# Layer 0's ConvFFN in five groups of channel tiles instead of six, and one more block-product pair in each layer of a two-layer encoder trunk

## The chip, the cores and the metric

The kernel runs on one core of a Trainium2 chip. A core has a matrix engine (TensorE; PE in the profile, its weight loads PEld), a vector engine (VectorE; DVE), a scalar engine (ScalarE; ACT), GpSimd (POOL), and SyncE (SP), whose queue issues every DMA here. Each engine runs its own instructions in order and waits on semaphores for the others. Operands lie in SBUF, 128 partitions wide; matmuls accumulate in PSUM, eight banks of 128 x 512 float32. The metric is the device time of one execution in microseconds; lower is better.

## The reference

A trunk of two layers over 512 positions of 1024 channels, in float32. Each layer has a mixing part (a Fourier group and a windowed attention group, projected back and added to x) and a ConvFFN. The change touches the ConvFFN alone:

```python
D_MODEL = 1024; SEQ = 512; DEPTH = 2; D_FF = 2816

def dwconv_centred(h, w, bias):
    hp = jnp.pad(h, ((0, 0), (1, 1), (0, 0)))
    return hp[:, :-2] * w[0] + hp[:, 1:-1] * w[1] + hp[:, 2:] * w[2] + bias

for l in range(DEPTH):
    ...
    x = x + mix @ w_o[l]
    h = rmsnorm(x, norm2[l])
    up = dwconv_centred(h @ w_up[l], conv_w[l], conv_b[l])
    gate, val = up[..., :D_FF], up[..., D_FF:]
    x = x + (jax.nn.silu(gate) * val) @ w_down[l]
```

## The kernel before

Everything is held transposed: channels on the 128 partitions, the 512 positions along the free dimension. x is eight tiles of 128 x 512 (KT = 8). The hidden width of 2816 is 22 channel tiles (FT = 22), each with a gate half and a value half.

**Precision by splitting.** A float32 operand is split into a rounded high part and the remainder (`split`, `wsplit`: ScalarE copies the high part at line 94, VectorE subtracts at line 97). `mm3` then issues three matmuls per product of a 128 x 128 weight block, at lines 124 (high, high), 125 (low, high) and 126 (high, low). Weights come by DMA from HBM into `wraw` buffers (three of 1024 columns) and are split into `whi` and `wlo` buffers (five each of up to 512 columns).

**The up projection of a channel tile, two ways.** `up_eight` takes the gate weights and the value weights one after the other: eight blocks each, every block against 512 positions, so 48 matmuls 512 wide. `up_seven` takes both halves together as a 2 x 2 block product in Strassen-Winograd form over the positions' halves and the channels' halves: seven products of four blocks against 256 positions, 84 matmuls 256 wide. Its sums on the position side (`seven_h`) are made once per layer. Its sums on the weight side (`s1` to `s4`) are made for each tile by VectorE, two of them in place in the `wraw` buffers. All seven weight operands are split, and PSUM parts are added up by VectorE. `SEVEN[l]` lists the tiles of layer l done this way; before, 7 in layer 0 and 12 in layer 1.

**After the up projection**, for each half: multiply by the row norm `rb2`, then `conv` (ScalarE scales and adds the bias, VectorE adds the two neighbour taps at line 100). Then SiLU on ScalarE, the product on VectorE, and a split into the pair `a`, kept in `gu`.

**The down projection** works on groups of channel tiles, `GROUPS[l]`. When a group's tiles are done, `rows` gives its eight rows, one for each tile of x: load the weights of this row and group, split, nf x 3 matmuls into one PSUM bank, add into x. A group of at most four loads two rows with one DMA; a larger group loads each row by itself and splits it in two pieces. The rows of one group run beside the up projections of the next, spread by `want`; of the rows beside the last group two are held back until its last tile is done. The rows of the last group come after everything else (the tail), and in layer 0 each also starts the next layer's norm.

**Where `gu` lies.** Four pairs fit in the four `slab` buffers, four in two `pT` buffers (2560 columns each), and in layer 1 four more in `m4`. A group's place is given by `c = fi % 8` in layer 0 and `fi % 12` in layer 1.

**Beside layer 0's ConvFFN** runs `presplit`: it splits layer 1's projection weights in advance and stores both parts in HBM (`kept`). `PIECES[fi]` says how many such pieces follow tile fi; four more calls lie in the tail.

**Order.** The program gives the order of the data and the buffers; a scheduler places the instructions of each engine from its own model of their times, so rows and up projections interleave matmul by matmul. Buffers of one tag go round, and a transfer into a buffer waits on SP's queue until its last reader is done.

Lines that the steps below use: 133 (`wload`'s DMA: up weights, and down weights of larger groups), 858 (the paired down loads), 167 (stores of the pre-split), 94 and 97 (splits and additions), 100 (taps), 124 to 126 (matmuls).

Of the kernel before, what the change touches and what calls it, by code (L numbers as in the profile page):

```python
# [9 lines left out]
F32R = mybir.dt.float32r  # L10
# [6 lines left out]
P = 128  # L17
# [15 lines left out]
RATE, STEP0 = 1, 12  # L33
FFN_BANKS = ("mm", "mm", "mm", "av", "sc", "sc")

GROUPS = ([(0, 4), (4, 4), (8, 4), (12, 3), (15, 3), (18, 4)], [(0, 4), (4, 6), (10, 6), (16, 6)])

PIECES = [1, 1, 2, 1, 2, 2, 2] + [1, 3] * 7 + [3]
SEVEN = ((7, 9, 11, 13, 15, 17, 19), (7, 8, 10, 11, 12, 14, 15, 16, 18, 19, 20, 21))


def encoder_kernel(tc, t):
# [25 lines left out]
    def nm(s):  # L68
        uid[0] += 1
        return f"{s}_{uid[0]}"  # L70

    def f(x):
        return x.bitcast(F32)
# [6 lines left out]
    def psum(tag="mm"):  # L80
        return ps.tile([P, 512], F32, tag=tag, name=nm("ps"), bufs=BANKS[tag])

    def temp(n, tag, dt=F32):
        size, bufs = TEMPS[tag]
        return tp.tile([P, size], dt, tag=tag, name=nm(tag), bufs=bufs)[:, :n]

    def pair(tag, n=512):
        return temp(2 * n, tag, F32R).rearrange("p (s q) -> p s q", s=2)

    def halves(z):  # L90
        return [z[:, s, :] for s in range(2)]

    def act(out, in_, func=AF.Copy, **kw):
        return nc.scalar.activation(out, in_, func, **kw)  # L94

    def tt(out, a, b, op, eng=None):
        return (eng or nc.vector).tensor_tensor(out, a, b, op=op)  # L97

    def stt(out, a, s, b, op0, op1):
        return nc.vector.scalar_tensor_tensor(out=out, in0=a, scalar=s, in1=b, op0=op0, op1=op1)  # L100

    def split(hi, lo, src, scale=None, eng=None):

        if scale is None:
            act(hi, src)
            tt(lo, src, f(hi), ALU.subtract, eng)
        else:
            act(hi, src, scale=scale)
            stt(lo, src, scale, f(hi), ALU.mult, ALU.subtract)
# [18 lines left out]
    def wtile():  # L128
        return wp.tile([P, 1024], F32, tag="wraw", name=nm("wraw"))

    def wload(src, n, raw=None):
        raw = wtile() if raw is None else raw
        nc.sync.dma_start(raw[:, :n], src)
        return raw[:, :n]

    def wsplit(raw, eng=None, hi_eng=None):
        hi = wp.tile([P, 512], F32R, tag="whi", name=nm("whi"), bufs=5)
        lo = wp.tile([P, 512], F32R, tag="wlo", name=nm("wlo"), bufs=5)
        n = raw.shape[-1]
        if hi_eng is None:  # L140
            act(hi[:, :n], raw)
        else:
            hi_eng.tensor_copy(hi[:, :n], raw)
        tt(lo[:, :n], raw, f(hi)[:, :n], ALU.subtract, eng)
        return hi, lo

    def wchunks(src, n, step=512, eng=None):
        raw = wload(src, n)
        return [wsplit(raw[:, c:min(c + step, n)], eng) for c in range(0, n, step)]
# [58 lines left out]
    def fetch(key, n=512):  # L208
        w = [wp.tile([P, 512], F32R, tag=z, name=nm(z), bufs=5) for z in ("whi", "wlo")]
        for o, z in zip(w, kept[key]):  # L210
            nc.sync.dma_start(f(o)[:, :n], z)
        return w
# [124 lines left out]
    def norm_tile(k, g, acc):  # L337

        a = pair("act")
        split(a[:, 0, :], a[:, 1, :], x[k], scale=g[:, k:k + 1])  # L340
        add_square(acc, x[k], k == 0)
        return a
# [14 lines left out]
    def fold_wu(raw, w=None):  # L357
        w = temp(512, "tA") if w is None else w
        fold(w, raw)
        return w  # L360

    def wwhole():
        return wp.tile([P, 512], F32, tag="whi", name=nm("whi"), bufs=5)

    def load_wf(l, j, raw=None):

        raw = wtile() if raw is None else raw
        nc.sync.dma_start(raw[:, :512].rearrange("p (z c) -> p z c", z=2),
                          t["w_fold"][l, j].rearrange("p (z c) -> p z c", z=2)[:, :, :256])
        return raw  # L370

    def fold_wf(raw, w=None):

        w = temp(512, "tA") if w is None else w
        tt(w[:, :256], raw[:, :256], raw[:, 256:512], ALU.add)
        tt(w[:, 256:], raw[:, :256], raw[:, 256:512], ALU.subtract)
        nc.vector.memset(w[:1, 256:384], 0.0)
        return w
# [110 lines left out]
    for l in range(L):  # L489
# [6 lines left out]
        for grp in (1, 0):  # L496
# [26 lines left out]
            z = temp(1536, "pT").rearrange("p (b c) -> p b c", b=NB)  # L523
            n = 256 if grp else 384
# [174 lines left out]
        for kk in range(KT // 2):  # L699
            if not l:  # L700
                wu = load_wu(l, kk)
            for k in (2 * kk, 2 * kk + 1):
                if k >= 4:
                    fold_h(k)
                w = fetch(f"u{k}") if l else [fold_wu(wu[k % 2], wwhole())]
# [4 lines left out]
                for m in (0, 1, 2, 3, 4) if l else (3, 4, 0, 1, 2):  # L710
                    if m < 3:
                        mm3(pee[m][:, :258], [z[:, m * P:(m + 1) * P] for z in h], we, st, sp_)
                    else:
                        c = (m - 3) * P
# [27 lines left out]
        for stage in range(2):  # L742
# [12 lines left out]
            for m in range(3):  # L755
                o = pe[m][:, :258]
                for i in range(2):
                    a, b = (ue, tabs) if stage == 0 else (tabs, ue)
# [18 lines left out]
        for j in range(NF):  # L777
# [3 lines left out]
            w = fetch(f"f{j}") if l else [fold_wf(load_wf(l, j), wwhole())]  # L781
# [16 lines left out]
        for j in range(NF):  # L798
            stt(yf[j], yf[j], gF[:, l, j:j + 1], rbF, ALU.mult, ALU.mult)
            a = pair("slab")  # L800
# [23 lines left out]
        for mp in range(KT // 2):  # L824
            for i, w in enumerate(wo(0, mp)):
                m = 2 * mp + i
# [5 lines left out]
        for mp in range(KT // 2):  # L832
            for i, w in enumerate(wo(1, mp)):
                m = 2 * mp + i
# [14 lines left out]
        def rows(f0, nf, gu):  # L849

            last = f0 + nf == FT
            for m in range(KT):
                if nf > 4:
                    w = wchunks(t["w_down"][l, m, :, f0 * P:(f0 + nf) * P], nf * P, step=nf * P // 2)
                else:
                    if m % 2 == 0:
                        raw = wtile()[:, :2 * nf * P].rearrange("p (m c) -> p m c", m=2)
                        nc.sync.dma_start(raw, t["w_down"][l, m:m + 2, :, f0 * P:(f0 + nf) * P].rearrange("m p c -> p m c"))
                    w = [wsplit(raw[:, m % 2, :])]
                kw = -(-nf // len(w))  # L860
                nh = 2 if last and l == L - 1 and m == KT - 1 else 1
                for h in range(nh):
                    q0, q1 = h * S // nh, (h + 1) * S // nh
                    nps[0] += 1
                    o = psum(FFN_BANKS[nps[0] % len(FFN_BANKS)])[:, q0:q1]
                    for k in range(nf):
                        mm3(o, [z[:, (k % kw) * P:(k % kw + 1) * P] for z in w[k // kw]],
                            [gu[k][:, s, q0:q1] for s in range(2)],
                            k == 0, k == nf - 1)
                    tt(x[m][:, q0:q1], x[m][:, q0:q1], o, ALU.add)  # L870
                    if last and l == L - 1:
                        nc.sync.dma_start(t["out"][m, :, q0:q1], x[m][:, q0:q1])
                if last and l < L - 1:
                    nxt.append(norm_tile(m, g1[:, l + 1, :], acc))
                yield

        down = iter(())
        for f0, nf in GROUPS[l]:
            gu = []

            todo = KT - 2 if f0 + nf == FT else KT
            done = 0
            for fi in range(f0, f0 + nf):
                ys_ = []
                for z, u in enumerate((up_seven if fi in SEVEN[l] else up_eight)(l, fi, h2, ts, rb2)):
                    ys_.append(conv(l, fi + z * FT, u))

                    n = 2 * (fi - f0) + z
                    want = -(-todo * (n + 2 - n % 2) // (2 * nf)) if n % 2 or n == 0 else done
                    if nf <= 4:  # L890
                        want = done + -(-(todo - done) // (2 * nf - n))
                    for _ in range(want - done):
                        next(down, None)
                    done = want
                if fi in (3, 4):
                    ts.append(seven_h(len(ts), h2, room))
                for _ in range(PIECES[fi]):
                    next(ahead)
                act(ys_[0], ys_[0], AF.Silu)
                tt(ys_[0], ys_[0], ys_[1], ALU.mult)  # L900
                c = fi % (12 if l else 8)
                if c < 4:
                    a = pair("slab")
                elif c < 8:
                    if c % 2 == 0:
                        two = temp(2048, "pT", F32R).rearrange("p (n s q) -> p n s q", n=2, s=2)
                    a = two[:, c % 2]
                else:
                    a = pair("m4")
                split(a[:, 0, :], a[:, 1, :], ys_[0])  # L910
                gu.append(a)
            for _ in down:
                pass
            down = rows(f0, nf, gu)
        if l < L - 1:
            acc = accum()
# [93 lines left out]
```

## Time and profile before

| what | us |
|---|---|
| median of three runs (lowest, highest) | 1039.85 (1039.72, 1041.09) |
| the profiled execution | 1039.14 |
| its span, first to last instruction | 1037.4 |
| granted TensorE clock | 1.000 |
| layer 0's ConvFFN, about | 192 to 537 |
| layer 1's ConvFFN, about | 706 to 1037 |

The span is a little shorter than the execution's time; what lies around it is 1.7 us. In the rows of the profile, an instruction's group is given by its line, engine, operation and tiles (out<-in), then the shape. In a timeline a row has its start, its duration, and in brackets the idle time of its engine before it and what ended it. A PE row lasts longer than the step to the next row, since matmuls overlap, so steps between starts are the thing to read.

### The profile page before, as it was taken

What the parts mean: (1) busy time and instruction counts of PE and PEld (TensorE: products, weight loads), DVE (VectorE), ACT (ScalarE), POOL (GpSimd) and SP (SyncE); (2) the same over time, 40 slices, a digit from 0 to 9 for tenths busy, and PEclk for the clock granted to TensorE, in tenths of its full rate; (3) what the DMA queues carried; (4) which work ended last, traced back from release to release, by engine and by line L of the source; (5) the groups of instructions that cost most, each with busy time, mean ns of one, the idle gap of its engine ahead of it and who ended that gap; (6) DMA issues with size and microseconds to landing.
All of it is one profiled execution on the core that took longest, in us unless ns stands there. A gap on an engine that the chain in (4) does not pass through costs nothing.

```text
span 1037.4 us, 16244 instructions
## 1 busy us (share of the span) xinstructions
PE 1024.4 (99%) x5774; PEld 891.1 (86%) x5774; DVE 862.5 (83%) x1747; ACT 545.8 (53%) x1068; POOL 60.6 (6%) x142
## 2 busy tenths in 40 slices
PE   8999999999999999999999999999999999999998
PEld 8887778888888888888899887888888898989987
DVE  8788749799998889999759876396999998999973
ACT  5338736455555455555544595254555555555631
POOL 0004410000000000000000063000000000000000
PEclk9999999999999999999999999999999999999999
DMA  7232122355564546567766422423224232333242
GB/s 275 87 106 72 44 91 82 117 172 179 163 206 145 193 175 204 186 221 231 240 212 200 151 62 84 141 82 102 82 73 137 82 107 85 104 112 101 68 149 85
DMA packets 62341, 140.15 MB, mean 135 GB/s; under 512 B 6450, under 2 KB 20018, under 8 KB 62260
## 3 DMA queue, kind: packets, MB, share of 16 engines
q1 hardware_dynamic: 62260, 139.12, 41.9%
q8 instruction: 45, 0.74, 0.3%
q14 instruction: 36, 0.29, 0.1%
HBM read 116.02 MB, written 23.07 MB: 134 GB/s over the span
## 4 chain that ended last, share of the span: by engine, by line
PE 92%; DVE 5%; ACT 1%; DMA 1%; issue 1%; POOL 0%; DVEq 0%; ACTq 0%
PE ps L124 27%; PE ps L126 27%; PE ps L125 27%; PE ps L122 3%; PE ps L680 2%; PE ps L673 2%; PE ps L661 1%; DVE tF L100 1%; DMA wraw<-in_w_up_dram 1%; DVE wlo L97 1%; DVE tA L665 1%; PE ps L242 1%; PE ps L235 1%; PE ps L621 0%; PE ps L282 0%
## 5 line engine op out<-in xcount | busy, mean ns | idle before, releaser
L94 ACT ACTIVATE whi<-wraw 128x512 fp32r<-128x512 f32 (+1 forms) x323 | 190.7, 603 | 222.2 <-PE ps L126 130.5
L97 DVE TENSOR_TENSOR wlo<-wraw,whi 128x512 fp32r<-128x512 f32 (+1 forms) x331 | 213.1, 657 | 48.6 <-ACT whi L94 47.7
L124 PE MATMUL ps<-act,whi 128*128 128x512 f32 (+1 forms) x692 | 244.9, 355 | 0.0
L125 PE MATMUL ps<-act,wlo 128*128 128x512 f32 (+1 forms) x692 | 244.4, 355 | 0.4 <-DVE wlo L97 0.3
L126 PE MATMUL ps<-act,whi 128*128 128x512 f32 (+1 forms) x692 | 244.1, 354 | 0.0
L125 PEld LDWEIGHTS ps<-act,wlo 128*128 128x128 f32 x692 | 130.6, 189 | 19.4 <-DVE wlo L97 0.9
L124 PEld LDWEIGHTS ps<-act,whi 128*128 128x128 f32 x692 | 130.6, 189 | 18.7
L126 PEld LDWEIGHTS ps<-act,whi 128*128 128x128 f32 x692 | 130.7, 189 | 18.0
L100 DVE SCALAR_TENSOR_TENSOR tF<-tF,pb,tF 128x511 f32<-128x511 f32 x176 | 130.2, 747 | 4.8 <-ACT tF L94 4.6
L97 DVE TENSOR_TENSOR x<-x,ps 128x512 f32<-128x512 f32 (+1 forms) x97 | 64.9, 677 | 34.9 <-PE ps L126 34.5
L124 PE MATMUL ps<-slab,whi 128*128 128x512 f32 (+1 forms) x240 | 93.1, 390 | 0.7 <-ACT whi L94 0.7
L125 PE MATMUL ps<-slab,wlo 128*128 128x512 f32 (+1 forms) x240 | 91.8, 383 | 0.0
L94 ACT ACTIVATE tF<-tF,pb 128x512 f32<-128x512 f32 x88 | 71.1, 810 | 37.7 <-DVE tF L97 37.1
L126 PE MATMUL ps<-slab,whi 128*128 128x512 f32 (+1 forms) x240 | 89.7, 384 | 0.0
L124 PE MATMUL ps<-room,whi 128*128 128x256 f32 x266 | 75.6, 284 | 0.5 <-DVE tF L97 0.2
L125 PE MATMUL ps<-room,wlo 128*128 128x256 f32 x266 | 75.0, 282 | 0.0
L126 PE MATMUL ps<-room,whi 128*128 128x256 f32 x266 | 74.9, 282 | 0.0
L97 DVE TENSOR_TENSOR tF<-ps,rb 128x512 f32<-128x512 f32 (+1 forms) x85 | 52.6, 627 | 15.3 <-ACT rb L94 11.0
L124 PE MATMUL ps<-pT,whi 128*128 128x512 f32 (+1 forms) x148 | 56.9, 384 | 0.0
L125 PE MATMUL ps<-pT,wlo 128*128 128x512 f32 (+1 forms) x148 | 56.8, 384 | 0.0
L126 PE MATMUL ps<-pT,whi 128*128 128x512 f32 (+1 forms) x148 | 56.1, 384 | 0.0
L124 PEld LDWEIGHTS ps<-slab,whi 128*128 128x128 f32 x240 | 45.1, 188 | 9.8 <-ACT whi L94 0.9
(206 smaller groups left out, 1923.9 us busy)
## 6 DMA issues: line engine op xcount, KB each, us to landing
wraw<-in_w_up_dram SPq DMA_DIRECT2D x88, 512.0 KB, 3.8
kept<-tA SPq DMA_DIRECT2D x56, 256.0 KB, 3.2
wraw<-in_w_down_dram SPq DMA_DIRECT2D x32, 384.0 KB, 3.8
wraw<-in_w_down_dram SPq DMA_DIRECT2D x20, 512.0 KB, 4.0
whi<-kept SPq DMA_DIRECT2D x28, 256.0 KB, 3.1
wlo<-kept SPq DMA_DIRECT2D x28, 256.0 KB, 3.0
kept<-tA SPq DMA_DIRECT2D x32, 192.0 KB, 1.9
wraw<-in_w_o_dram SPq DMA_DIRECT2D x8, 512.0 KB, 4.3
```

The source lines that it names most:

```text
L94: return nc.scalar.activation(out, in_, func, **kw)
L97: return (eng or nc.vector).tensor_tensor(out, a, b, op=op)
L100: return nc.vector.scalar_tensor_tensor(out=out, in0=a, scalar=s, in1=b, op0=op0, op1=op1)
L122: nc.tensor.matmul(out, a[0], b[0], start=start, stop=stop, **kw)
L124: nc.tensor.matmul(out, a[0], b[0], start=start, stop=False, **kw)
L125: nc.tensor.matmul(out, a[1], b[0], start=False, stop=False, **kw)
L126: nc.tensor.matmul(out, a[0], b[1], start=False, stop=stop, **kw)
L235: nc.tensor.matmul(pt[:, 2 * b:2 * b + 2], acc[:, b * P:(b + 1) * P], ones2, start=True, stop=True)
L242: nc.tensor.matmul(pt[:, b * P:(b + 1) * P], r[:, b:b + 1].to_broadcast([P, P]), ident, start=True, stop=True)
L661: nc.tensor.matmul(sc[:, :n], qT[p][:, e, i * P:(i + 1) * P], kT[g][:, s, j0 * P:(j1 + 1) * P], start=s == 0, stop=s == 1)
L673: tr = nc.tensor.transpose(pp[:, j * P:(j + 1) * P], pr[:, j * P:(j + 1) * P], ident)
L680: pv = nc.tensor.matmul(py[64 * e:64 * e + 64, i0 * P:(i1 + 1) * P], vp[:, j, 64 * g:64 * g + 64], pT[:, half, e, b0:b0 + 2 * (i1 - i0) + ...
```

## The change

Layer 0's ConvFFN has the groups 4, 5, 4, 5, 4 in place of 4, 4, 4, 3, 3, 4, so five sets of eight down rows and not six. A row of a group of five is loaded alone (640 columns) and split as 384 and 256; the step of 384 is what groups of six had already. Tile 21 of layer 0 becomes an eighth block product, and layer 1 has thirteen instead of twelve, in other places: 7 to 9, 11 to 14 and 16 to 21, where it was 7, 8, 10 to 12, 14 to 16 and 18 to 21. Layer 0's places go by `fi % 9`: the two `pT` buffers are taken together at c == 4, hold four pairs, and the fifth pair of a group lies in the last 512 columns of both. After tile 21 two pieces of the pre-split follow and not three, so that one moves into the tail. The reads of `gu` take a list of two parts in place of one array.

```diff
-GROUPS = ([(0, 4), (4, 4), (8, 4), (12, 3), (15, 3), (18, 4)], [(0, 4), (4, 6), (10, 6), (16, 6)])
-
-PIECES = [1, 1, 2, 1, 2, 2, 2] + [1, 3] * 7 + [3]
-SEVEN = ((7, 9, 11, 13, 15, 17, 19), (7, 8, 10, 11, 12, 14, 15, 16, 18, 19, 20, 21))
+GROUPS = ([(0, 4), (4, 5), (9, 4), (13, 5), (18, 4)], [(0, 4), (4, 6), (10, 6), (16, 6)])
+
+PIECES = [1, 1, 2, 1, 2, 2, 2] + [1, 3] * 7 + [2]
+SEVEN = ((7, 9, 11, 13, 15, 17, 19, 21), (7, 8, 9, 11, 12, 13, 14, 16, 17, 18, 19, 20, 21))
...
                 if nf > 4:
-                    w = wchunks(t["w_down"][l, m, :, f0 * P:(f0 + nf) * P], nf * P, step=nf * P // 2)
+                    w = wchunks(t["w_down"][l, m, :, f0 * P:(f0 + nf) * P], nf * P, step=3 * P)
...
                         mm3(o, [z[:, (k % kw) * P:(k % kw + 1) * P] for z in w[k // kw]],
-                            [gu[k][:, s, q0:q1] for s in range(2)],
+                            [z[:, q0:q1] for z in gu[k]],
                             k == 0, k == nf - 1)
...
-                c = fi % (12 if l else 8)
+                c = fi % (12 if l else 9)
+                if c == 4:
+
+                    big = [temp(2560, "pT", F32R) for _ in range(2)]
                 if c < 4:
-                    a = pair("slab")
+                    a = halves(pair("slab"))
                 elif c < 8:
-                    if c % 2 == 0:
-                        two = temp(2048, "pT", F32R).rearrange("p (n s q) -> p n s q", n=2, s=2)
-                    a = two[:, c % 2]
+                    a = [big[c // 6][:, (2 * (c % 2) + s) * 512:(2 * (c % 2) + s + 1) * 512] for s in range(2)]
+                elif l == 0:
+                    a = [z[:, 2048:2560] for z in big]
                 else:
-                    a = pair("m4")
-                split(a[:, 0, :], a[:, 1, :], ys_[0])
+                    a = halves(pair("m4"))
+                split(*a, ys_[0])
                 gu.append(a)
```

## The prediction

> **What bounds the kernel now.** I read the busy shares and the chain first, then windows over the ConvFFN of both layers, then single rows of TensorE and VectorE. From the page, the engines' busy line and the chain of work that ended last:
>
> ```profile
> PE 1024.4 (99%) x5774; PEld 891.1 (86%) x5774; DVE 862.5 (83%) x1747; ACT 545.8 (53%) x1068; POOL 60.6 (6%) x142
> PE 92%; DVE 5%; ACT 1%; DMA 1%; issue 1%; POOL 0%; DVEq 0%; ACTq 0%
> ```
>
> TensorE holds 92% of the chain. The question is what it waits for inside the ConvFFN, the only part that the change touches. The windows (us; busy time of PE, PEld, DVE, ACT, POOL; clock; DMA share; GB/s) are layer 0's ConvFFN up to its last channel tile, its tail, and layer 1's tiles 18 to 21:
>
> ```profile
> 195.00:506.00 311.00, 310.14 (x1645) 268.00 (x1644) 285.16 (x510) 170.04 (x299) 0.00 (x0) 1.00 0.57 188
> 505.00:538.00 33.00, 32.87 (x164) 28.80 (x162) 23.12 (x38) 16.34 (x27) 1.10 (x6) 1.00 0.66 216
> 936.53:998.84 62.31, 62.19 (x427) 57.65 (x427) 57.56 (x105) 34.71 (x66) 0.00 (x0) 1.00 0.35 106
> ```
>
> TensorE is full in all three, at the full clock. VectorE is nearly full too: 285.16 of 311.00 us is 92%, and the same 92% in the last row. So there are two limits close together: the matmuls set the time, and VectorE may take over wherever it gets more work than the matmuls beside it cover. A busy PE hides short waits (a row lasts longer than its step to the next), so I count from start to start. Timeline of PE, wide and then narrow matmuls; 35 rows and 17 rows:
>
> ```profile
> 761.51 0.39 PE L125 MATMUL ps<-act,wlo 128*128 128x512 f32 x1
> ...
> 769.22 0.39 PE L126 MATMUL ps<-slab,whi 128*128 128x512 f32 x1
> ...
> 772.42 0.28 PE L125 MATMUL ps<-act,wlo 128*128 128x256 f32 x1
> ...
> 774.33 0.28 PE L126 MATMUL ps<-room,whi 128*128 128x256 f32 x1
> ```
>
> A wide matmul takes (769.22 - 761.51) / 34 = 0.2268 us, a narrow one (774.33 - 772.42) / 16 = 0.1194 us. A step much above these is a stall. Two of layer 0, then the five of layer 1:
>
> ```profile
> 269.50 0.39 PE L124 MATMUL ps<-slab,whi 128*128 128x512 f32 x1
> 270.01 0.38 PE L124 MATMUL ps<-room,whi 128*128 128x256 f32 x1
> ...
> 370.91 0.38 PE L124 MATMUL ps<-act,whi 128*128 128x256 f32 x1
> 371.95 0.49 PE L124 MATMUL ps<-slab,whi 128*128 128x512 f32 x1 [0.66 <-ACT whi L94]
> 372.52 0.39 PE L125 MATMUL ps<-act,wlo 128*128 128x256 f32 x1
> 372.74 0.28 PE L126 MATMUL ps<-act,whi 128*128 128x256 f32 x1
> ...
> 775.18 0.29 PE L124 MATMUL ps<-act,whi 128*128 128x256 f32 x1
> 775.74 0.38 PE L125 MATMUL ps<-act,wlo 128*128 128x256 f32 x1 [0.28 <-DVE wlo L97]
> ...
> 786.93 0.28 PE L124 MATMUL ps<-act,whi 128*128 128x256 f32 x1
> 787.45 0.39 PE L124 MATMUL ps<-room,whi 128*128 128x256 f32 x1 [0.24 <-DVE tF L97]
> ...
> 953.84 0.28 PE L126 MATMUL ps<-room,whi 128*128 128x256 f32 x1
> 954.24 0.38 PE L124 MATMUL ps<-room,whi 128*128 128x256 f32 x1
> ...
> 979.76 0.28 PE L124 MATMUL ps<-act,whi 128*128 128x256 f32 x1
> 980.03 0.39 PE L124 MATMUL ps<-room,whi 128*128 128x256 f32 x1
> ...
> 984.32 0.29 PE L124 MATMUL ps<-act,whi 128*128 128x256 f32 x1
> 984.61 0.50 PE L124 MATMUL ps<-m,whi 128*128 128x512 f32 x1
> ```
>
> At 370.91 the steps are 1.04, 0.57 and 0.22 us, which is 0.92 + 0.34 + 0.10 = 1.4 us lost; at 269.50 the step of 0.51 loses 0.3, with the 0.23 behind it 0.4. In layer 1 the five steps are 0.56, 0.52, 0.40, 0.27 and 0.29 long, so 0.44 + 0.40 + 0.28 + 0.15 + 0.17 = 1.4 us over 0.12, and with 0.10 in the step behind each 1.9 us. Two of these fall at tiles 7 and 8, three in the run of four block products 18 to 21 (0.9 us, 0.23 per tile). The stalls name splits (whi, wlo) and VectorE sums: weights that are not ready.
>
> **The change, part by part. Matmuls.** An ordinary pair is 2 x 8 x 3 = 48 wide matmuls, 48 x 0.2268 = 10.89 us. A block-product pair is 7 x 4 x 3 = 84 narrow ones, 84 x 0.1194 = 10.03 us. Each layer gets one more of these: 2 x 0.86 = **1.7 us** less TensorE time, on the path because TensorE is full. Regrouping alters no matmul: 22 tiles times 8 rows times 3 stay.
>
> [...]
>
> **VectorE's price of it.** Start to start on the DVE timeline:
>
> ```profile
> 945.08 0.68 DVE L97 TENSOR_TENSOR wlo<-wraw,whi 128x512 fp32r<-128x512 f32 x1
> 945.68 0.68 DVE L97 TENSOR_TENSOR wraw<-wraw 128x512 f32<-128x512 f32 x1
> ...
> 946.89 0.41 DVE L97 TENSOR_TENSOR tF<-tF,ps 128x256 f32<-128x256 f32 x1
> 947.22 0.75 DVE L100 SCALAR_TENSOR_TENSOR tF<-tF,pb,tF 128x511 f32<-128x511 f32 x1
> 947.88 0.69 DVE L97 TENSOR_TENSOR wlo<-wraw,whi 128x512 fp32r<-128x512 f32 x1
> ...
> 956.22 0.55 DVE L97 TENSOR_TENSOR wlo<-wraw,whi 128x384 fp32r<-128x384 f32 x1
> 956.68 0.68 DVE L97 TENSOR_TENSOR tF<-tF,tF 128x512 f32<-128x512 f32 x1
> ```
>
> So 0.60 for 512 columns, 0.46 for 384, 0.33 for 256, 0.66 for a convolution tap. An ordinary pair has 8 of the first (four weight splits, two scalings, product, last split) and 4 taps: 4.8 + 2.6 = 7.4 us. A block product has 14 (four sums, seven splits, scaling, product, last split), 5 of 256 and 4 taps: 8.4 + 1.7 + 2.6 = 12.7 us. Each conversion adds 5.3 us to VectorE, while TensorE gets shorter. ScalarE's additional splits and copies lie on an engine that is 53% busy.
>
> Layer 1, tile by tile. Beside tiles 16 to 21 runs about one down row of six channel tiles per tile: 18 wide matmuls, 4.08 us, and 2 x 0.46 + 0.60 = 1.5 us of VectorE. A block product there needs 10.03 + 4.08 = 14.1 us of TensorE and 14.2 of VectorE: about even, and the trace loses 0.23 per tile. The run grows from 18-21 to 16-21, two more at 0.23: **+0.5 us**. Beside tiles 4 to 9 run 8 rows of four over six tiles: 8 x 12 x 0.2268 / 6 = 3.6 us, VectorE 8 x 1.2 / 6 = 1.6. A block product has 13.7 against 14.3: 0.6 short. Tile 9 now follows 7 and 8 as a third: **+0.6 us**. Beside 10 to 15 the row share is 5.4 us against 2.0, so 15.5 against 14.7: covered, and the run 11 to 14 costs nothing. So layer 1 gives back about 1.1 of its 0.86: between 0 (the scheduler fills gaps) and 2 us.
>
> Layer 0. Five groups instead of six drop 8 additions into x, 8 x 0.60 = 4.8 us of VectorE. Splits go from 32 of 512 and 16 of 384 (19.2 + 7.4 = 26.6 us) to 24 of 512, 16 of 384 and 16 of 256 (14.4 + 7.4 + 5.3 = 27.1). Net 4.3 us less VectorE work in 311. Only stalls can turn this into time: 1.4 us at 370.91 and 0.4 at 269.50. The first falls at tile 13, beside rows of the old groups of three. In the new group 13 to 17 the three block products have 10.03 + 4.4 = 14.4 us of TensorE against 12.7 + 1.9 + 0.6 (one piece for the next layer) = 15.2, but the two ordinary tiles between have 15.2 against 7.4 + 1.9 + 1.8 = 11.1: 73.6 against 67.8 together, so no lasting shortage, though a local stall can appear. I take **-0.6 us**, between -1.8 (both stalls go) and +1.5 (one more like 370.91).
>
> Tile 21 of layer 0 as a block product sits before the tail. There VectorE has 23.12 of 33.00 us. Its last split ends at 511.7, and VectorE then waits for TensorE:
>
> ```profile
> 511.06 0.68 DVE L97 TENSOR_TENSOR pT<-tF,pT 128x512 fp32r<-128x512 f32 x1
> 516.17 2.48 DVE L97 TENSOR_TENSOR x<-x,ps 128x512 f32<-128x512 f32 x4 [4.43 <-PE ps L126]
> ```
>
> The 5.3 us more are partly met by this 4.4 us gap, and the two rows held back become 2 x 15 x 0.2268 = 6.8 us of cover instead of 2 x 9 x 0.2268 = 4.1. One piece of the pre-split (0.6 us on VectorE, its two stores on SP) moves from tile 21 into the same slack; if that cover failed it would cost its 0.6 us. Allocating both pT buffers at once (c == 4) waits for the previous group's rows, which are emptied before that tile begins: nothing, and 1 us at most if they ran late.
>
> Transfers. Layer 0's down weights went in 16 loads of 512 KB and 8 of 384; now 12 of 512 and 16 of 320. From the list of DMA issues (count, size, us to landing), and the waits of layer 0 (total, times, longest), ScalarE's and SP's:
>
> ```profile
> wraw<-in_w_down_dram SPq DMA_DIRECT2D x32, 384.0 KB, 3.8
> wraw<-in_w_down_dram SPq DMA_DIRECT2D x20, 512.0 KB, 4.0
> ...
> ACT whi L94 <- DMA wraw<-in_w_up_dram: 25.7, 13, 5.4
> ...
> SPq L133 <- DVE wlo L97: 57.9, 23, 6.2
> ```
>
> A 320 KB load should land in about 3.7 us (my estimate from the two sizes). A row of five holds one of three wraw buffers; a row pair held one for two rows, hence longer. I price it at nothing, covered by matmuls in the queue, and keep its failure as a rival.
>
> **Sum** on the profiled execution (1039.14 us, span 1037.4): -1.7 + 1.1 - 0.6 = -1.2, so 1037.9. The median shown, 1039.85, lies 0.7 above that execution; against it the same sum gives **1038.7 us**.
>
> **Rivals.** (1) The whole matmul gain and layer 0's relief arrive, and layer 1 hides its extra VectorE work in VectorE's idle 8%: -1.7 - 1.7 + 0.2 = -3.2, so 1036.6. For it: VectorE has 4.7 us idle in 936.53 to 998.84. Against: stalls sit exactly there. (2) VectorE takes all back: layer 1 +1.9, layer 0 unchanged: 1040.0. For it: even balance in both runs. (3) Slower: the wraw buffers. Beside tiles 9-12 and 18-21 each row now takes a load of its own; a block product holds two buffers almost to its end, so rows and the next tile's weights share the third, and SP, serving in order, holds the next up load behind a row's load that waits for a buffer. ScalarE's mean wait for an up load is 25.7 / 13 = 2.0 us. It decides once that wait outlasts the split weights TensorE still has queued; with two such waits reaching it in two of the four block products there, +4.0 on the forecast: 1042.7. Against it: SP's waits in layer 0 end with almost no stall now, and single rows in layer 1 run the same way. [...]
>
> **Chances.** About 0.2% (2.1 us) is what a measurement tells from no change. Forecast 0.42 (its own range 1037.6 to 1039.7), rival 1 0.28, rival 2 0.20, rival 3 0.10. Faster by over 0.2% (below 1037.8) is rival 1 and a little of the forecast: 0.32. Slower (above 1041.9): 0.10. The rest, 0.58, is within. The range takes rivals 1 and 2 with the stall bounds: 1036.0 to 1041.0.
>
> **What would show it.** The counts would show 168 narrow matmuls more and 96 wide ones fewer. Right: steps at layer 1's tiles 9 and 16-21 above 0.12 us, ending on wlo, whi or VectorE sums, adding about 1 us; no 1.4 us step near layer 0's tile 13; layer 0's ConvFFN shorter by 1 to 2 us. Wrong: stalls in layer 0 that end on in_w_up or in_w_down loads (rival 3), or layer 1 shorter by the full 0.86 (rival 1).

## The result, and the profile after

The changed kernel is slower: median 1054.18 us (1053.77 to 1056.23, four runs) against 1039.90 us of the kernel before in the same runs, a ratio of 1.0138 [1.0126, 1.0151]. The forecast was 1038.7 and the range ended at 1041.0. The profiled execution is 1053.77 us long, its span 1051.9.

From the page of the changed kernel, the engines' busy line and the chain that ended last:

```profile
PE 1027.7 (98%) x5846; PEld 894.2 (85%) x5846; DVE 870.5 (83%) x1769; ACT 553.4 (53%) x1088; POOL 60.3 (6%) x142
PE 79%; DVE 15%; DMA 4%; ACT 1%; issue 1%; POOL 0%; DVEq 0%; ACTq 0%
```

VectorE's share of the chain went from 5% to 15% and DMA's from 1% to 4%. To see where, I cut both spans at the row-norm matmuls (line 235) that open each ConvFFN. Windows view (us; then busy us and count of PE, PEld, DVE, ACT, POOL; granted clock; DMA share; GB/s) of the changed kernel, layer 1's ConvFFN and then layer 0's:

```profile
707.60:1051.90 344.30, 331.30 (x1979) 294.31 (x1977) 286.58 (x500) 167.42 (x302) 1.01 (x1) 1.00 0.31 94
191.50:539.70 348.20, 345.19 (x1851) 299.63 (x1850) 312.24 (x560) 192.57 (x338) 2.90 (x7) 1.00 0.59 191
```

The same view of the kernel before:

```profile
705.00:1037.40 332.40, 328.63 (x1943) 292.50 (x1941) 281.83 (x489) 166.29 (x296) 1.01 (x1) 1.00 0.32 98
191.30:537.30 346.00, 345.01 (x1817) 298.48 (x1815) 308.69 (x549) 186.00 (x324) 2.50 (x7) 1.00 0.58 191
```

Layer 0's ConvFFN is 2.2 us longer (348.2 against 346.0), layer 1's 11.9 us (344.3 against 332.4). The clock is full in all four. In layer 1 TensorE is idle for 344.3 - 331.3 = 13.0 us, where it was idle for 3.8. So the matmuls did not get slower; they wait.

For what, the waits of both kernels between 710 and 1030 us say (engine, instruction and releaser: us in total, times, longest). The changed kernel:

```profile
ACT whi L94 <- DVE wraw L97: 36.2, 17, 3.6
...
DVE sums L97 <- DMA wraw<-in_w_up_dram: 11.4, 11, 2.7
...
PE ps L124 <- DVE tF L97: 6.5, 7, 1.5
```

The kernel before:

```profile
ACT whi L94 <- DVE wraw L97: 16.3, 12, 2.5
...
DVE sums L97 <- DMA wraw<-in_w_up_dram: 3.0, 7, 0.6
...
PE ps L124 <- DVE tF L97: 0.2, 1, 0.2
```

VectorE's first operation of a block product (sums) waits four times as long for its up weights, ScalarE's splits then wait for VectorE, and TensorE at the end for VectorE. One tile shows the whole chain. Timeline of PE in the changed kernel, in the run 16 to 21, with its largest step:

```profile
973.20 0.28 PE L124 MATMUL ps<-act,whi 128*128 128x256 f32 x1
973.88 0.39 PE L125 MATMUL ps<-act,wlo 128*128 128x256 f32 x1 [0.40 <-DVE wlo L97]
...
978.05 0.28 PE L126 MATMUL ps<-act,whi 128*128 128x256 f32 x1
979.80 0.39 PE L124 MATMUL ps<-room,whi 128*128 128x256 f32 x1 [1.47 <-DVE tF L97]
```

The steps are 0.68 and 1.75 us where 0.12 is due: 0.56 and 1.63 us lost. The second ends when VectorE empties a PSUM part. VectorE's timeline there:

```profile
966.57 0.68 DVE L97 TENSOR_TENSOR tF<-tF,tF 128x512 f32<-128x512 f32 x1
969.92 0.69 DVE L97 TENSOR_TENSOR sums<-wraw,wraw 128x512 f32<-128x512 f32 x1 [2.68 <-DMA wraw<-in_w_up_dram]
...
979.34 0.41 DVE L97 TENSOR_TENSOR tF<-ps,rb 128x256 f32<-128x256 f32 x1
979.67 0.68 DVE L97 TENSOR_TENSOR wlo<-wraw,whi 128x512 fp32r<-128x512 f32 x1
```

It stood idle for 2.68 us before the tile's up weights came, and from 969.92 on has no idle time at all; what TensorE waits for stands in that queue and comes at 979.34. SP's queue says why the weights were late. Up loads of three successive tiles (x2: gate and value), the changed kernel:

```profile
947.21 1.53 SPq L133 DMA_DIRECT2D wraw<-in_w_up_dram  x2
...
963.01 1.53 SPq L133 DMA_DIRECT2D wraw<-in_w_up_dram  x2
971.11 0.33 SPq L133 DMA_DIRECT2D wraw<-in_w_down_dram  x1
980.38 1.53 SPq L133 DMA_DIRECT2D wraw<-in_w_up_dram  x2
```

The next tile's loads go out at 980.38, 0.03 us after the split that began at 979.67 ends and leaves `wraw` (979.67 + 0.68 = 980.35). This is a loop: 963.01 to 969.92 for the transfers until the sums can start (6.9 us), 969.92 to 980.35 for VectorE's queue (10.4 us), then the next load. In the 6.9 us lies about 1.2 us for which the second of the two loads, which the sums need too, waits for its own buffer (the row of both issues spans 1.53 us, a single issue 0.33). This turn takes 17.4 us, the one before it 15.8 (947.21 to 963.01); TensorE needs 14.1.

### The profile page after: what moved, and what is told of

Its sections match the earlier page's. It is cut to its first block, busy times and chain, and to the rows that moved or that the text cites. A ratio compares the mean times of both kernels' runs of the same rounds, so it can differ in the third digit from the quotient of the medians.

```text
span 1051.9 us, 16451 instructions
## 1 busy us (share of the span) xinstructions
PE 1027.7 (98%) x5846; PEld 894.2 (85%) x5846; DVE 870.5 (83%) x1769; ACT 553.4 (53%) x1088; POOL 60.3 (6%) x142
## 4 chain that ended last, share of the span: by engine, by line
PE 79%; DVE 15%; DMA 4%; ACT 1%; issue 1%; POOL 0%; DVEq 0%; ACTq 0%
PE ps L124 24%; PE ps L126 24%; PE ps L125 24%; DVE wlo L97 4%; DMA wraw<-in_w_up_dram 3%; DVE tF L100 2%; PE ps L680 2%; PE ps L673 2%; DVE tF L97 1%; PE ps L661 1%; DVE sums L97 1%; DVE wraw L97 1%; DVE act L97 1%; PE ps L122 1%; DVE x L97 1%
## 5 line engine op out<-in xcount | busy, mean ns | idle before, releaser
L94 ACT ACTIVATE whi<-wraw 128x512 fp32r<-128x512 f32 (+2 forms) x333 | 194.5, 594 | 243.9 <-PE ps L126 162.1
L97 DVE TENSOR_TENSOR wlo<-wraw,whi 128x512 fp32r<-128x512 f32 (+2 forms) x341 | 216.2, 643 | 45.7 <-ACT whi L94 44.1
L124 PE MATMUL ps<-act,whi 128*128 128x512 f32 (+1 forms) x684 | 239.5, 351 | 1.0 <-ACT whi L94 1.0
L125 PE MATMUL ps<-act,wlo 128*128 128x512 f32 (+1 forms) x684 | 239.0, 351 | 1.0 <-DVE wlo L97 1.0
L126 PE MATMUL ps<-act,whi 128*128 128x512 f32 (+1 forms) x684 | 238.5, 350 | 0.0
L124 PE MATMUL ps<-room,whi 128*128 128x256 f32 x294 | 84.8, 288 | 8.6 <-DVE tF L97 6.5
L97 DVE TENSOR_TENSOR x<-x,ps 128x512 f32<-128x512 f32 (+1 forms) x89 | 59.6, 675 | 30.1 <-PE ps L126 29.9
L125 PE MATMUL ps<-room,wlo 128*128 128x256 f32 x294 | 83.1, 282 | 0.5 <-DVE wlo L97 0.5
L126 PE MATMUL ps<-room,whi 128*128 128x256 f32 x294 | 82.9, 282 | 0.0
L124 PEld LDWEIGHTS ps<-room,whi 128*128 128x128 f32 x294 | 55.8, 190 | 12.6 <-DVE tF L97 7.0
L125 PEld LDWEIGHTS ps<-room,wlo 128*128 128x128 f32 x294 | 55.8, 190 | 1.9 <-DVE wlo L97 0.7
L126 PE MATMUL ps<-pT,whi 128*128 128x512 f32 (+1 forms) x148 | 56.8, 384 | 0.0
```

The costliest lines, as they stand in the source:

```text
L124: nc.tensor.matmul(out, a[0], b[0], start=start, stop=False, **kw)
L125: nc.tensor.matmul(out, a[1], b[0], start=False, stop=False, **kw)
L126: nc.tensor.matmul(out, a[0], b[1], start=False, stop=stop, **kw)
```

## The experiments

All ratios are medians against the kernel before in the same runs, with a 95% interval. "Layer 1" is the profiled length from line 235 to the end of the span (before 332.4, after 344.3). My theory after the result: the loss of layer 1 is that loop, three `wraw` buffers with VectorE's order in it, which a short run of block products outlives on weights loaded ahead. Rivals: VectorE simply has too much work; the new places of `gu` or the groups of layer 0 shift something later.

**Layer 1's list put back, layer 0 as changed.**

```diff
-SEVEN = ((7, 9, 11, 13, 15, 17, 19, 21), (7, 8, 9, 11, 12, 13, 14, 16, 17, 18, 19, 20, 21))
+SEVEN = ((7, 9, 11, 13, 15, 17, 19, 21), (7, 8, 10, 11, 12, 14, 15, 16, 18, 19, 20, 21))
```

> The changed kernel with layer 1's twelve block products where they were before; all else as changed. Theories for layer 1: (ring) three wraw buffers make a closed loop of load, sums, splits and release that is longer than a block-product tile's matmuls, paid once per tile of a long run; (throughput) VectorE simply has too much work in such runs; (storage) the new way of taking the pT buffers changed the order of layer 1's instructions. Ring and throughput: layer 1 as before, 331 to 333 us from its first up matmul, and the whole 2 to 3 us above before (layer 0's part): 1042 to 1043. Storage: layer 1 stays long, 1047 or more.

Measured 1044.24 us, 1.0042 [1.0027, 1.0057]; layer 1 is 332.9 us, as before. The new groups and the storage do nothing to layer 1. What is left, some 4 us, is layer 0's; about 1.5 us of it is a stretch at half clock (all four runs have a mean granted clock of 0.998; last section).

**Only layer 1's list changed, on the kernel before.** The edit is the second tuple of `SEVEN` alone.

> The kernel before with nothing changed but layer 1's list of thirteen. Ring and throughput: nearly the whole loss of layer 1, some 12 us, so 1050 to 1053. Storage: 1039 to 1041.

Measured 1051.24 us, 1.0102 [1.0085, 1.0119]; layer 1 is 346.0 us in the profiled execution, whose mean granted clock is 0.998 where the three other runs have 1.000 (last section). The list alone costs 11 us.

**The long run broken.** Tile 17 of layer 1 is made ordinary, so that 18 to 21 follow an ordinary tile as in the kernel before, and twelve block products are left.

```diff
-(7, 8, 9, 11, 12, 13, 14, 16, 17, 18, 19, 20, 21)
+(7, 8, 9, 11, 12, 13, 14, 16, 18, 19, 20, 21)
```

> The changed kernel with tile 17 of layer 1 an ordinary pair again, so twelve block products: 7 to 9, 11 to 14, 16, 18 to 21. Ring and throughput: of the 10 us of stalls in tiles 16 to 21 at most 2 remain, while those at 8, 9, 11 and 12 (about 6 us) stay: 1045 to 1047. If the number of block products mattered and not the run: 1053.

Measured 1049.02 us, 1.009 [1.0075, 1.0105], above what I had set, since layer 0 lost about 4 us in this run too. Layer 1 is 337.8 us: 6.5 less than after. Tiles 18 to 21 lose 1.8 us by their steps; in the changed kernel tiles 18 to 20 alone lose about 6. Tiles 8, 9, 12 and 13 keep their 5 us (counted by the sums of each tile, the stalls that the expectation puts at 11 and 12 lie in 12 and 13). A block product has no fixed price: the same four tiles are cheap behind an ordinary one and dear behind two of their own kind.

**Rows off the ring.** The rows of groups of six load into `m4` instead of `wraw` (`wchunks` gets the argument `raw` for it).

```diff
-w = wchunks(..., step=3 * P)
+w = wchunks(..., step=3 * P, raw=temp(1024, "m4") if l else None)
```

> The changed kernel; in layer 1 the rows of groups of six load their down weights into a free m4 buffer, so that the three wraw buffers serve up weights alone. VectorE's work is the same. Ring: the next tile's first load starts earlier, VectorE's waits for up weights go, and most of layer 1's 15 us of stalls with them: 1041 to 1046. Throughput: no change, 1053 to 1056.

Measured 1063.61 us, 1.0227 [1.0211, 1.0242]. As a test of the total this failed: `m4` also holds four pairs of `gu`, and the rows now fight with these. Its waits between 710 and 1030 us:

```profile
ACT whi L94 <- DMA m<-in_w_down_dram: 13.9, 4, 4.1
...
ACT m L94 <- DVE tF L97: 9.1, 3, 4.5
...
DVE sums L97 <- DMA wraw<-in_w_up_dram: 3.0, 6, 1.3
```

The last row is the useful one: VectorE's wait for up weights fell from 11.4 to 3.0 us, and tiles 16 to 20 lost 2.8 us by their steps and not 7.1. So the rows' share of the ring is part of the loop, though not to be had this way.

**A fourth `wraw` buffer**, paid for with two of six `tA` buffers, on the changed kernel, and the same on the kernel before as its control.

```diff
-             "tA": (512, 6), "tF": (512, 6), "sq": (512, 2)}
+             "tA": (512, 4), "tF": (512, 6), "sq": (512, 2)}
...
-        return wp.tile([P, 1024], F32, tag="wraw", name=nm("wraw"))
+        return wp.tile([P, 1024], F32, tag="wraw", name=nm("wraw"), bufs=4)
```

> The changed kernel with four wraw buffers instead of three; the room comes from tA (four buffers instead of six), which layer 1's ConvFFN does not use. The work is the same. Ring: in layer 1's long runs a next tile's weights can land while the two of this tile are held, VectorE's waits for up weights go, and layer 1's 16 us of stalls fall under 5: layer 1 from its first up matmul 332 to 337 us instead of 344 to 346, the whole 1041 to 1046. Throughput: layer 1 stays at 343 to 346, the whole 1051 to 1056.

> The kernel before with four wraw buffers, the room from tA as in the run with four wraw buffers of the changed kernel (e5), so that the two differ by the change alone. Layer 1 330.5 to 332.5 us against 336.4 there; about 1.5 to 2 us lost outside the ConvFFN by the smaller tA: 1039.5 to 1042.

On the changed kernel: 1047.60 us, 1.0065 [1.005, 1.008], layer 1 336.4 us. On the kernel before: 1042.61 us, 1.0027 [1.0016, 1.0038], layer 1 333.0 us, a little above what I had set for both. The buffer takes 7.9 of the 11.9 us off the new list and nothing off the old one. In layer 0's ConvFFN it takes off 1.4 us (346.8 against 348.2) and 1.5 us (344.5 against 346.0). The fewer `tA` buffers cost about 3 us outside the ConvFFNs in the first run and 4 in the second, which is why the first total lies above my numbers while its layer 1 does not. The waits of the changed kernel with four buffers, 710 to 1030 us:

```profile
ACT whi L94 <- DVE wraw L97: 15.6, 10, 2.6
...
DVE sums L97 <- DMA wraw<-in_w_up_dram: 3.0, 6, 1.1
```

Both are back at what the kernel before shows. About 3.4 us (336.4 against 333.0) is left.

**A tap less.** Tiles done as block products in layer 1 leave out the left tap of the convolution: 2 x 0.66 = 1.3 us less VectorE work a tile. First with three buffers, then with four.

```diff
+        if not (l and m % FT in SEVEN[l]):
-        stt(y[:, 1:], u[:, :-1], cw[:, l, 0, m:m + 1], y[:, 1:], ALU.mult, ALU.add)
+            stt(y[:, 1:], u[:, :-1], cw[:, l, 0, m:m + 1], y[:, 1:], ALU.mult, ALU.add)
```

> The changed kernel without the left tap of the convolution in layer 1's thirteen block-product tiles: 26 taps of 0.66 us fewer on VectorE, 1.3 us per tile. The matmuls and loads are the same. Throughput: 12.9 us of VectorE against 14.1 of TensorE, so layer 1's stalls nearly vanish, below 3 of 16 us: 1039 to 1042. Ring: the loop of some 16.3 us per tile shortens by at most those 1.3 us and stays above 14.1, so 5 to 9 us of stalls remain: 1044 to 1049.

> The changed kernel with four wraw buffers (tA four) and without the left tap in layer 1's thirteen block-product tiles. If the ring of three buffers and VectorE's even balance are the whole of layer 1's loss, nothing is left to wait for: layer 1 from its first row-norm matmul 331 to 333 us (before 332.4, changed 344.3), stalls in tiles 16 to 21 under 1 us. If something else costs there (order, PSUM banks), it stays above 334.

Three buffers: 1043.10 us, 1.0024 [1.0015, 1.0034], layer 1 333.0 us. The total lies between the numbers of the two theories; the stalls that stay, 3 us, are fewer than the 5 to 9 that the loop left in my expectation. This run alone does not tell the two apart, since the tap is a part of the loop too. With four: 1041.94 us, 1.0019 [1.001, 1.0028], layer 1 330.7 us, no stall left in tiles 16 to 21. The windows view over most of the run 16 to 21 puts it in one row each. With four buffers and the tap left out:

```profile
917.00:1000.00 83.00, 83.00 (x581) 77.95 (x580) 74.14 (x135) 49.21 (x91) 0.00 (x0) 1.00 0.35 104
```

With four buffers alone:

```profile
917.00:1000.00 83.00, 80.56 (x562) 74.93 (x561) 78.80 (x143) 47.07 (x88) 0.00 (x0) 1.00 0.34 99
```

The changed kernel:

```profile
917.00:1000.00 83.00, 76.71 (x540) 71.00 (x540) 73.75 (x134) 43.67 (x84) 0.00 (x0) 1.00 0.31 95
```

In the changed kernel both engines have idle time: TensorE 6.3 of 83 us, VectorE 9.2. Neither is the limit; the loop between them is. With the buffer VectorE fills to 78.8 of 83 us, 95%, and nearly is the limit. With the tap gone as well TensorE has no idle time. So the 7.9 us that the buffer takes off, with VectorE's work as it was, are the loop's, and the last 3.4 us go only when VectorE has less to do. The tap alone takes off 11.3 us (344.3 to 333.0): it shortens the loop as well, so the two shares can't be added.

**Four buffers on the kernel before, paid for with `m4`** (five to four buffers).

> The kernel before with four wraw buffers, the room from m4 (four instead of five). Candidate for better than both. Ring: the 0.9 us in tiles 18 to 21 and part of the 1.0 at 7 and 8 go, unless m4 costs it back in the attention part: 1038 to 1040.5. If buffers did not matter there: 1040 to 1041.

1049.90 us, 1.0092 [1.0076, 1.0107]; layer 1 is 333.0 us, and the loss of 10 us lies outside it. Neither of the two places tried for the buffer is cheap.

**Layer 0: the groups alone** (seven block products there, three pieces at tile 21, layer 1 as before), and **tile 21 alone** (on the kernel before, with two pieces).

```diff
-SEVEN = ((7, 9, 11, 13, 15, 17, 19, 21), (7, 8, 9, 11, 12, 13, 14, 16, 17, 18, 19, 20, 21))
+SEVEN = ((7, 9, 11, 13, 15, 17, 19), (7, 8, 10, 11, 12, 14, 15, 16, 18, 19, 20, 21))
```

```diff
-SEVEN = ((7, 9, 11, 13, 15, 17, 19), ...
+SEVEN = ((7, 9, 11, 13, 15, 17, 19, 21), ...
```

> Of the change only layer 0's groups (and the places of the pairs): layer 0 keeps its seven block products and its pieces, layer 1 its twelve. With the other part of layer 0 (the next run) it splits the 4 us that layer 0 lost. If the new spread of the rows causes the stalls at tiles 6 and 7 (2.5 to 4 us): 1042 to 1044. If they come from elsewhere: 1038 to 1040, as the prediction's layer-0 step had it.

> The kernel before with tile 21 of layer 0 as a block product and one piece fewer behind it, nothing else. By the prediction's sum the matmul gain of 0.9 us arrives, since the tail covers VectorE's 5.3 us: 1039. If the tail does not cover them, the rows of the last group wait: 1041 to 1043.

Groups alone: 1042.02 us, 1.0016 [1.0006, 1.0027], with a wide spread (1039.45 to 1044.38). Tile 21 alone: 1040.96 us, 1.0005 [0.9996, 1.0014]: the 0.86 us of matmuls are not gained. Neither part does anything good by itself.

The groups bring new stalls where tile 7 begins. Changed kernel, timeline of PE:

```profile
266.74 0.28 PE L126 MATMUL ps<-sq,whi 128*128 128x256 f32 x1
268.01 0.38 PE L124 MATMUL ps<-act,whi 128*128 128x256 f32 x1 [0.99 <-ACT whi L94]
268.53 0.38 PE L124 MATMUL ps<-room,whi 128*128 128x256 f32 x1
269.57 0.50 PE L124 MATMUL ps<-slab,whi 128*128 128x512 f32 x1 [0.65 <-ACT whi L94]
```

Steps of 1.27, 0.52 and 1.04 us: 1.15 + 0.40 + 0.92 us over 0.12. ScalarE at that point:

```profile
267.06 0.38 ACT L94 ACTIVATE tF<-ps 128x256 f32<-128x256 f32 x1 [2.38 <-PE ps L126]
267.34 0.62 ACT L94 ACTIVATE whi<-wraw 128x512 fp32r<-128x512 f32 x1
```

ScalarE stood for 2.38 us at a copy out of PSUM that needs TensorE's matmul of 266.74, while the split that TensorE needs next stood behind it in the same queue. The two engines wait for each other in turn. In tile 21's case TensorE runs dry before that tile's own pair is made. The kernel before with tile 21 alone, PE:

```profile
514.64 0.39 PE L126 MATMUL ps<-pT,whi 128*128 128x512 f32 x1
516.68 0.50 PE L124 MATMUL ps<-pT,whi 128*128 128x512 f32 x1 [1.65 <-ACT pT L94]
```

A step of 2.04 us, 1.81 over 0.23, up to the split of the tile's product; with 0.27, 0.51 and 0.11 from 520.2 to 521.5, 2.7 us in this tail.

**Tile 21 in place of tile 7** (layer 0's groups as changed, list 9 to 21, layer 1 as before).

```diff
-SEVEN = ((7, 9, 11, 13, 15, 17, 19, 21), ...
+SEVEN = ((9, 11, 13, 15, 17, 19, 21), ...
```

> The changed kernel with layer 1's old list, and in layer 0 tile 7 an ordinary pair, so seven block products: 9 to 21, every second. VectorE has no idle time in tiles 1 to 6 of the changed layer 0. If the 2.5 to 4 us of stalls at tiles 6 and 7 come from a first block product met with VectorE behind, they go, for 0.9 us more of matmuls: 1040.5 to 1042, against 1044.2 with tile 7. If the groups' rows cause them, they move to tile 9 and the time stays at 1044 to 1045.

Measured 1039.54 us, 0.9996 [0.9987, 1.0005]: no difference from the kernel before, and 4.7 us less than with tile 7 (about 1.5 of them the stretch at half clock: the mean granted clock is 0.998 there and 1.000 in all ten runs here). The stalls at 267 to 270 us are gone and do not come back at tile 9; the tail's 1.9 us stay. This is the best version I found, and it is not faster than the kernel before.

## Why the prediction was wrong

**What bounds the kernel.** Right that two limits lie close together. Wrong in what the five small stalls of layer 1 were taken for: 0.23 us a tile in the run 18 to 21 was read as the price of a block product beside those rows.

**Matmuls, -1.7 us.** Right in the count and the steps: layer 1 has 1979 - 1943 = 36 more, as 84 for 48 makes, and the steps are the same: in the changed kernel 0.2267 us for a wide matmul (24 steps, 718.08 to 723.52 us) and 0.1193 for a narrow one (15 steps, 974.22 to 976.01). With the waits taken away (four buffers and no left tap), layer 1 takes 330.7 us, 1.7 below the kernel before: the 0.86 and most of its old stalls. Taking the steps from the rows was right.

**VectorE's price, 5.3 us a conversion.** Near: layer 1's busy time went up by 286.58 - 281.83 = 4.75 us.

**Layer 1, +1.1 us: the step that failed.** It measured +0.86 + 11.9 = 12.8. Its three parts, by their steps:

- "two more at 0.23: +0.5": the run 16 to 21 loses 8.8 us where 18 to 21 lost 0.9, so 7.9 more.
- "+0.6" for tiles 7 to 9: 3.6 us of stalls there, where 7 and 8 had 1.0, so 2.6 more.
- "covered, and the run 11 to 14 costs nothing": 2.1 us at tiles 12 and 13.

Together 12.6 of the 12.8 us. The mistake is the same in each: I compared sums of work a tile (14.1 against 14.2 us), and took a stall per tile from a short run. The row that I should have read was there. VectorE's first sums of the run, kernel before (tiles 18, 19, 20 and 21):

```profile
927.65 0.69 DVE L97 TENSOR_TENSOR sums<-wraw,wraw 128x512 f32<-128x512 f32 x1 [0.17 <-DMA wraw<-in_w_up_dram]
...
943.87 0.69 DVE L97 TENSOR_TENSOR sums<-wraw,wraw 128x512 f32<-128x512 f32 x1 [0.55 <-DMA wraw<-in_w_up_dram]
...
959.89 0.69 DVE L97 TENSOR_TENSOR sums<-wraw,wraw 128x512 f32<-128x512 f32 x1
...
975.54 0.69 DVE L97 TENSOR_TENSOR sums<-wraw,wraw 128x512 f32<-128x512 f32 x1 [0.59 <-DMA wraw<-in_w_up_dram]
```

They lie 16.2, 16.0 and 15.7 us apart, while TensorE got through a tile in about 14.1. The loop was slower than TensorE already then, by some 2 us a tile, 5.6 us over the three turns; weights made ready beside the ordinary tile 17 can pay for that, and the run ended in time. In the changed kernel tile 16 loses nothing, 17 loses 0.8 us, and each tile from 18 on 1.4 to 2.9. Its sums of tiles 18, 19 and 20:

```profile
937.22 0.69 DVE L97 TENSOR_TENSOR sums<-wraw,wraw 128x512 f32<-128x512 f32 x1 [1.32 <-DMA wraw<-in_w_up_dram]
...
953.02 0.69 DVE L97 TENSOR_TENSOR sums<-wraw,wraw 128x512 f32<-128x512 f32 x1 [1.32 <-DMA wraw<-in_w_up_dram]
...
969.92 0.69 DVE L97 TENSOR_TENSOR sums<-wraw,wraw 128x512 f32<-128x512 f32 x1 [2.68 <-DMA wraw<-in_w_up_dram]
```

They lie 15.8 and 16.9 us apart, and TensorE now takes as long for a tile. From tile 17 to 21 a turn takes 15.8 us on average, no longer than the 16.0 of tiles 18 to 21 before; with the fourth buffer it takes 15.0, without the tap 14.6, with both 14.3. So the loop itself is shown by the rows and by these runs. That the lead is what runs out fits the broken run, but is not shown alone, because VectorE's order differs too. In its tiles 20 and 21 the kernel before subtracts for a tile's first weights ahead of the tile's sums (21, whose sums are the row at 975.54):

```profile
972.84 0.63 ACT L94 ACTIVATE whi<-wraw 128x512 fp32r<-128x512 f32 x1 [0.63 <-DMA wraw<-in_w_up_dram]
...
973.66 0.69 DVE L97 TENSOR_TENSOR wlo<-wraw,whi 128x512 fp32r<-128x512 f32 x1
```

The changed kernel does it behind the sums (20, sums at 969.92):

```profile
967.92 0.63 ACT L94 ACTIVATE whi<-wraw 128x512 fp32r<-128x512 f32 x1
...
973.14 0.68 DVE L97 TENSOR_TENSOR wlo<-wraw,whi 128x512 fp32r<-128x512 f32 x1
```

Here ScalarE's high part was done at 968.55, and VectorE stood idle until 969.92 because the sums, which need the second load too, came first in its queue. The subtraction began 4.6 us after the high part, and TensorE's step of 0.68 us at 973.20 waits for it. The scheduler makes this order. The broken run has the order of the kernel before again in tiles 19 to 21, and no run changed the order alone: how much of the loss is the order's stays open.

**Layer 0, -0.6 us, and tile 21 at nothing.** Both failed. The stall of 1.4 us at tile 13 did go, as said. But the step looked for a shortage in the group 13 to 17 alone. Beside tiles 4 to 8 the rows of the first four tiles now spread over five tiles: 8 x 12 x 0.2268 / 5 = 4.4 us of cover a tile, where it was 5.4, and tile 7 loses 2.5 us. Tile 7 as a block product is needed for it, as the exchange with tile 21 shows; that the thinner cover is the reason is argued, not shown. For tile 21 I counted VectorE's idle 4.4 us before the tail as cover. It was VectorE waiting for TensorE; with the tile's product later, TensorE waits for it instead, 1.9 us in the tail of the changed kernel (the run with the groups alone, where tile 21 is ordinary, has no such stall). There, four additions into x stand ahead of the next low parts on VectorE:

```profile
518.82 2.48 DVE L97 TENSOR_TENSOR x<-x,ps 128x512 f32<-128x512 f32 x4 [2.45 <-PE ps L126]
521.22 0.68 DVE L97 TENSOR_TENSOR wlo<-wraw,whi 128x512 fp32r<-128x512 f32 x1
```

and TensorE's next row that multiplies by a low part of these, at 522.25, needs this wlo (done at 521.90). The row that ends the stall, at 522.00, belongs to the next layer's projections (whi,act) and doesn't read it. The profile puts its wait to this wlo here, and in the run with layer 1's list put back the same step to the load of the pre-split weights (`whi<-kept`), so which of the two ends it is open, and so is how much of the 1.9 us another order would save. Layer 0's sum by the steps: -0.86, and stalls of 2.6 at tile 7, 0.7 at tile 17 and 1.9 in the tail, 5.2 us, where 0.4 + 1.4 + 0.4 = 2.2 were, so +2.1; measured +2.2.

**Transfers at nothing.** In layer 0 right as far as up and down weights go: none of its stalls ends on one of their loads. The 320 KB loads landed in 4.0 us (median), where 3.7 was the estimate.

**The rivals.** Rival 3 named the mechanism, a block product holding two `wraw` buffers and rows sharing the third until the wait outlasts the weights still queued. It had 0.10 and stood in layer 0 beside rows of five. I put it aside because "single rows in layer 1 run the same way": they did, in runs too short for the loss to show. Rivals 1 and 2 held VectorE's amount of work to be the only question, and so the range ended 13 us short.

## What to carry to other kernels

For work that loops through a ring of buffers, measure the period of the loop, from one load into the ring to the next, and set it against the bound engine's time for an iteration; stalls of a short run say little of a longer one when that period is the larger. An engine's idle time next to the changed work is cover only if it isn't waiting for the engine that is to be covered; here VectorE's 4.43 us before layer 0's tail were such a wait. Where two engines have equal work per iteration, ask whether the buffers between them suffice: here three cost 12 us with VectorE's work even with TensorE's, and about 3 us of stalls with 1.3 us a tile less of it.

## What the runs showed of the hardware

In some executions TensorE ran at a lower granted clock for a few microseconds after short gaps, in others not. In the kernel with the groups alone, the stalls at tile 7 are followed by such a stretch; windows view, 3.5 us with the stalls and twice 3.5 us behind them (the granted clock is the third figure from the end):

```profile
266.80:270.30 3.50, 1.72 (x9) 1.06 (x8) 2.77 (x5) 2.46 (x5) 0.00 (x0) 1.00 0.75 210
270.30:273.80 3.50, 3.50 (x20) 3.50 (x19) 2.44 (x5) 1.54 (x3) 0.00 (x0) 0.53 0.96 294
273.80:277.30 3.50, 3.50 (x18) 2.95 (x18) 2.88 (x7) 2.01 (x4) 0.00 (x0) 0.98 0.36 143
```

The profiled execution of the changed kernel has the same stalls and no drop:

```profile
266.80:270.30 3.50, 1.72 (x9) 1.07 (x9) 2.77 (x5) 2.46 (x5) 0.00 (x0) 1.00 0.73 196
270.30:273.80 3.50, 3.50 (x27) 3.28 (x26) 3.06 (x6) 1.85 (x3) 0.00 (x0) 1.00 0.93 351
273.80:277.30 3.50, 3.50 (x17) 2.90 (x16) 3.16 (x7) 1.91 (x4) 0.00 (x0) 1.00 0.20 83
```

In the first, narrow matmuls step by 0.21 us and not 0.12, and 20 are done where 27 were. The longest step before it is 1.27 us, and TensorE was busy for 1.72 of the 3.50 us ahead. Behind the stalls the windows lose (0.47 + 0.02) x 3.5 = 1.7 us of full clock; an estimate from these two, with half clock throughout, is a stretch of 3.4 us. With layer 1's list put back, narrow matmuls in the profiled execution step by 0.12 us up to 271.67 and by 0.21 from there to 274.44, where the view ends. The mean granted clock of the profiled execution is 0.998 in both and also with only layer 1's list changed, and 0.994, the lowest of all, with the rows off the ring. What sets off the drop is not shown: the same stalls have it behind them in one execution and not in another.

A drop costs about 1.5 us: with the same layer 0, its ConvFFN took 349.7 us with the drop (layer 1's list put back) and 348.2 without (the changed kernel), near the 1.7 us of clock that the windows lose. So the stalls at tile 7 cost more in some executions than in others. Of the ten executions of the groups alone, the two with a mean granted clock of 1.000 took 1039.45 and 1040.57 us, the eight with 0.998 took 1041.43 to 1044.38; 3.4 us at half clock make 0.998 of the mean. That bears out that the drop is a part of their wide spread; the 3 us among the eight it doesn't explain.
